# The compression's weight units between those of the queries' projection, and the first chunk's gates handed to the attention's list of side work

## The chip, the cores and the metric

One Trainium2 chip, and one of its cores. The metric is device time in microseconds (us) of one execution of the whole program. The kernel before has a median of 2008.77 us over 3 runs.

## What is computed

One step of a decoder layer with the same weights for two groups: a prompt of 1024 tokens, and 8 sequences of 8 new tokens each over a paged cache of 2048 (the sample). Width is 1024; all is float32. Cut to what the change touches, for the prompt:

```
h   = rmsnorm(x) * (1 + scale) + shift
zq, zk, zv, za, zr, zqn, zkv, zg = split(h @ w_in)     # one input projection
o_g = rmsnorm(gla(zq, zk, zv, za)) * silu(zr)          # gated linear attention, zr are its gates
kc  = silu(windows(zkv[0]) @ w1[0] + b1) @ w2[0] + b2  # compression: 63 blocks of 32 tokens
vc  = silu(windows(zkv[1]) @ w1[1] + b1) @ w2[1] + b2
o_n = g0 * attn(zqn, kc, vc) + g1 * attn(zqn, selected k, v) + g2 * attn(zqn, window k, v)
x   = x + gt * rmsnorm(concat(o_g, o_n) @ w_out)       # then a squared-ReLU MLP
```

## The kernel before

Tokens lie on the free axis, in three chunks: 384, 384 and 256 prompt tokens with the 64 sample tokens (`CHUNKS`). Each float32 operand of a product is split into a high part, rounded by ScalarE (`split`, L248), and the rest, subtracted by VectorE (L249). A product is then three matmuls (`mm3`, L254 to L256).

Weights come in units of 512 KB (`wunit`, L261). SyncE (SP in the profile) loads a unit into one of 3 buffers `wr`; ScalarE makes `wh` and VectorE `wl`, each with 2 buffers. So a `wh` buffer is free again when TensorE has ended the unit before last, and a `wr` buffer when the `wl` of its unit is made. SP works in order: a load that waits for a buffer holds all loads behind it.

The program is written stage by stage, and the compiler's scheduler then fixes one order for each engine. `main_phase` calls in turn:

- `project_kv`: keys and values of the three branches, written to DRAM (`kvd`, `vd`). At its end POOL starts two copies of the sample's window state from DRAM to DRAM (L803, L804).
- `keys_values`: first the compression. For each kind (keys, values) it loads one row of `kvd` (L1024), splits it, and multiplies it with 4 weight units `cw1` of 12 matmuls each into one accumulator in PSUM's `mm` banks. A tanh, two transposes and a small product make `KC` and `VC`. Then it loads the keys and values of the other two branches (`k32`, `v32`, one buffer each, L1081 and L1085) and splits them into `KK` and `VV`.
- `project_q`: 4 units `w_f`, each over the three chunks (72 matmuls), written to `qd`.
- `project_gate`: 4 units over chunks two and three (48 matmuls each), then the same 4 units, loaded again, over chunk one (24 each). Each result passes a tanh (L760) and two VectorE operations (L761, L763) that multiply it into `catg`; POOL writes that to DRAM (`cgd`).
- `attention`: prompt tiles of 128 tokens in 16 passes. For each of the 8 heads TensorE makes scores against `KC`, `KK[1]` and `KK[0]` (L1122, L1123), VectorE adds the mask and takes the maximum (L1125), ScalarE the exponential (L1129), POOL scales (L1135), TensorE transposes (L1145) and multiplies with the values (L1148, L1149).

While the attention runs, a generator (`sample`) gives side work: the sample's own attention, in `SAMPLE_WORK` = 122 steps over the first three of four parts, as many as the done share of the attention's width asks for:

```python
while done < min(1, work / total(i)) * STEPS[i == 3]:
    done += next(between, 1e9)
```

Of the kernel before, what the change touches and what calls it, by code (L numbers as in the profile page):

```python
# [17 lines left out]
NP = 1024  # L18
# [9 lines left out]
SAMPLE_WORK = 10 + 4 * 28  # L28
# [188 lines left out]
class Prog:  # L217
# [320 lines left out]
    def hidden(self, i):  # L538
        c0, npr, n = CHUNKS[i]
        hp = self.pool(self.right, f"hT{c0}", side="right")  # L540
        self.xs.append(tuple(self.t(hp, [128, 8, n], F32R, f"hT{k}") for k in range(2)))
# [74 lines left out]
    def main_phase(self):  # L616
        nc, tc, a = self.nc, self.tc, self.a
        ffn = ExitStack()
        with ExitStack() as top:
            with ExitStack() as left, self.right as right:  # L620
                self.catg = self.t(self.pool(right, "cat", side="right"), [128, 4, NT], F32, "catg")
# [10 lines left out]
                next(project_gla)  # L632
                for i in (1, 2):
                    self.hidden(i)
# [21 lines left out]
            between, work, done = self.sample(), 0, 0  # L656
# [97 lines left out]
    def project_gate(self, pool, xs):  # L754
        nc, a = self.nc, self.a

        for cis, i in product((slice(1, 3), slice(0, 1)), range(4)):
            for ps, (c0, npr, n) in zip(self.feat_linear(a["w_f"][4 + i], 128, xs[cis]), CHUNKS[cis]):
# [3 lines left out]
                cat = self.catg[:, i, c0:c0 + n]  # L762
# [12 lines left out]

# [46 lines left out]
    def gla(self, st):  # L822
# [11 lines left out]
        for i in range(8):  # L834
# [75 lines left out]
            nc.scalar.mul(self.catg[:, :, cols], pt.rearrange("p (h t) -> p h t", h=4), self.small[:, 32:33])  # L910
# [18 lines left out]
    def gla_sample(self, pool):  # L929
# [52 lines left out]
        nc.vector.scalar_tensor_tensor(self.catg[:, :, NP:], v(oT), self.small[:, 32:33], v(r), op0=OP.mult, op1=OP.mult)  # L982
# [27 lines left out]
    def keys_values(self, st):  # L1010
# [6 lines left out]
        with ExitStack() as st2:  # L1017
            pool = self.pool(st2, "cmp")
            t = lambda shape, tag, bufs=1, dt=F32: self.t(pool, shape, dt, tag, bufs)
            nb = 63  # L1020
            M = 2 * nb
            for kind in range(2):
                x32 = t([128, NP], "x32", 2)
                nc.sync.dma_start(x32, self.kvd[kind, :, :NP])  # L1024
                xh, xl = (t([128, 8, 64, 2], x, 1, F32R) for x in ("xh", "xl"))
                for h in range(2):
                    for j2 in range(2):
                        src = x32[64 * h:64 * h + 64].rearrange("p (c j i) -> p i j c", j=8, i=2)[:, j2]
                        self.split(*(y[64 * j2:64 * j2 + 64, :, :, h] for y in (xh, xl)), src)
                ps = self.bank("mm")[:M, :256]  # L1030
                xs = [y.rearrange("p j c h -> p j (c h)") for y in (xh, xl)]
                for u in range(4):
                    h, l = self.wunit(a["cw1"][kind, u], 4, 256)
                    for i in range(4):
                        k = 4 * u + i
                        o = 2 * (k // 8)
                        self.mm3(ps, (xs[0][:, k % 8, o:o + M], xs[1][:, k % 8, o:o + M]), (h[:, i], l[:, i]),
                                 k == 0, False)
                nc.tensor.matmul(ps, self.C("ones")[:3, :M], self.brow[:, kind], start=False, stop=True)
                e = t([128, 256], "ce", 2)[:M]  # L1040
                nc.scalar.activation(e, ps, AF.Tanh, scale=0.5)
                nc.vector.scalar_tensor_tensor(e, e, 1.0, ps, op0=OP.add, op1=OP.mult)
                nc.vector.tensor_scalar(e, e, 0.5, None, op0=OP.mult)
                pt = self.bank("g")[:, :2 * M].rearrange("p (a b) -> p a b", a=2)
                for f in range(2):
                    nc.tensor.transpose(pt[:, f], e[:, f * 128:(f + 1) * 128], self.C("ident")[:M, :M])
                hh, hl = (t([128, 2, M], x, 2, F32R) for x in ("chh", "chl"))
                self.split(hh, hl, pt)
                if kind == 0:
                    pk = self.bank("g")[:, :M]  # L1050
                    for f in range(2):
                        self.mm3(pk, (self.cw2h[:, 0, f], self.cw2l[:, 0, f]), (hh[:, f], hl[:, f]), f == 0, f == 1)
                    b2 = self.small[:, 33:34]
                    for h in range(2):
                        src = pk.rearrange("p (c h) -> p h c", h=2)[:, h]
                        dst = self.KC[:, h, :, :nb]
                        nc.vector.tensor_scalar(dst[:, 0], src, b2, None, op0=OP.add)
# [513 lines left out]
```

## Time and profile before

| | |
|---|---|
| median of 3 runs | 2008.77 us (2002.26 to 2010.27) |
| profiled execution, its own time | 2006.12 us |
| its span, first to last instruction | 2004.5 us |
| mean granted clock of TensorE | 0.952 of full speed |
| TensorE busy | 1864.0 us (93% of the span) |
| VectorE busy | 1111.7 us (55%) |
| ScalarE busy | 799.0 us (40%) |
| POOL busy | 410.8 us (20%) |

How to read it: a busy TensorE is not one at full speed. Its granted clock has two levels, 1.2 and 2.4 GHz, which the views show as 0.50 and 1.00; a value between is a mean over a stretch with both. Idle time of any engine costs something only where TensorE, or the engine that bounds that stretch, waits for it. PE is TensorE's matmul, DVE VectorE, ACT ScalarE, SPq SyncE's issue of transfers.

### The profile page before, as it was taken

The page shows a single profiled execution, that of the slowest core. Times are in us where ns is not written, and L with a number is a line of the kernel's source. Part 1 is how long each engine was busy: PE and PEld are TensorE (multiplying, and loading weights), DVE is VectorE, ACT ScalarE, POOL GpSimd, SP SyncE. Part 2 cuts the span into 40 slices and gives each one's busy share as a digit, 9 for nine tenths or more (in the row PEclk, how much of TensorE's full clock was granted, in tenths as well). Part 3 has the DMA queues.
Part 4 walks back from the last instruction along what each step waited for, and adds up shares of the span by engine and source line. Part 5 has one row for each costly group of instructions (what it writes and reads, how often), then busy time and mean ns, then how long its engine had stood idle before and what let it go on. Part 6 is the DMA issues. An engine that isn't in the chain of part 4 may idle for free.

```text
span 2004.5 us, 33005 instructions
## 1 busy us (share of the span) xinstructions
PE 1864.0 (93%) x12033; PEld 1711.5 (85%) x12033; DVE 1111.7 (55%) x2493; ACT 799.0 (40%) x1646; POOL 410.8 (20%) x660
## 2 busy tenths in 40 slices
PE   4989999999979989999998879999999999999995
PEld 3878889999969866576796878989999999999995
DVE  7757765364533596677768757633333333333347
ACT  4324353253332475566756635432302121212153
POOL 3433202134401344444312013000000000000024
PEclk9999999999969898899999889999999999999998
DMA  7567641013543503333212476551111111111125
GB/s 248 177 223 252 208 129 53 22 38 123 176 166 119 173 6 97 108 108 106 80 53 69 151 226 221 199 172 63 43 42 53 43 43 43 48 48 43 43 76 176
DMA packets 107624, 223.93 MB, mean 112 GB/s; under 512 B 12763, under 2 KB 68477, under 8 KB 106022
## 3 DMA queue, kind: packets, MB, share of 16 engines
q1 hardware_dynamic: 91814, 172.07, 26.9%
q0 software_dynamic: 13920, 47.53, 7.0%
q8 instruction: 94, 1.54, 0.3%
q10 hardware_dynamic: 1728, 2.23, 0.3%
q14 instruction: 68, 0.56, 0.1%
HBM read 190.72 MB, written 35.19 MB: 113 GB/s over the span
## 4 chain that ended last, share of the span: by engine, by line
PE 76%; DVE 10%; DMA 6%; issue 3%; ACT 2%; POOL 1%; SPq 1%; POOLq 0%; ACTq 0%; DVEq 0%
PE mm L255 13%; PE mm L254 13%; PE mm L256 13%; PE dn L254 6%; PE dn L255 6%; PE dn L256 6%; PE g L1145 3%; DMA wr<-w_ada 2%; PE av L1148 2%; PE dn L1122 2%; PE av L1149 2%; PE dn L1123 1%; DVE wl L249 1%; PE g L882 1%; PE mm L1296 1%
## 5 line engine op out<-in xcount | busy, mean ns | idle before, releaser
L248 ACT CAST wh<-wr 128x1024 fp32r<-128x1024 f32 (+1 forms) x152 | 158.2, 1041 | 444.7 <-PE dn L255 273.1
L249 DVE TENSOR_TENSOR wl<-wr,wh 128x1024 fp32r<-128x1024 f32 (+1 forms) x144 | 177.6, 1234 | 205.5 <-ACT wh L248 205.2
L254 PE MATMUL mm<-fh,wh 128*128 128x384 f32 (+1 forms) x768 | 254.1, 331 | 13.0 <-DMA fh<-h2d 13.0
L254 PE MATMUL dn<-fh,wh 128*128 128x384 f32 (+1 forms) x768 | 253.9, 332 | 7.3 <-DVE fo L1513 3.4
L255 PE MATMUL mm<-fl,wh 128*128 128x384 f32 (+1 forms) x768 | 254.5, 331 | 3.3 <-DMA fl<-h2d 3.3
L256 PE MATMUL mm<-fh,wl 128*128 128x384 f32 (+1 forms) x768 | 253.1, 331 | 1.6 <-DVE wl L249 1.1
L255 PE MATMUL dn<-fl,wh 128*128 128x384 f32 (+1 forms) x768 | 253.4, 330 | 0.1
L256 PE MATMUL dn<-fh,wl 128*128 128x384 f32 (+1 forms) x768 | 252.7, 330 | 0.0
L1513 DVE TENSOR_TENSOR fo<-fo,dn 128x384 f32<-128x384 f32 (+1 forms) x168 | 88.9, 530 | 190.7 <-PE dn L256 189.8
L254 PEld LDWEIGHTS mm<-fh,wh 128*128 128x128 f32 x768 | 145.6, 190 | 13.5 <-issue 12.0
L254 PEld LDWEIGHTS dn<-fh,wh 128*128 128x128 f32 x768 | 144.4, 188 | 10.9 <-ACT fh L248 4.6
L551 POOL TENSOR_TENSOR acc<-acc,sq 128x384 f32<-128x384 f32 x14 | 18.7, 1338 | 653.9 <-ACT sq L550 653.6
L255 PEld LDWEIGHTS mm<-fl,wh 128*128 128x128 f32 x768 | 145.5, 189 | 4.1 <-DMA fl<-h2d 4.1
L256 PEld LDWEIGHTS mm<-fh,wl 128*128 128x128 f32 x768 | 145.5, 190 | 2.2 <-DVE wl L249 1.4
L255 PEld LDWEIGHTS dn<-fl,wh 128*128 128x128 f32 x768 | 144.7, 188 | 1.2 <-DVE fl L249 1.2
L256 PEld LDWEIGHTS dn<-fh,wl 128*128 128x128 f32 x768 | 144.6, 188 | 0.0
L254 PE MATMUL mm<-hT,wh 128*128 128x384 f32 (+3 forms) x408 | 138.0, 338 | 1.8 <-ACT st L771 1.8
L255 PE MATMUL mm<-hT,wh 128*128 128x384 f32 (+3 forms) x408 | 136.9, 336 | 0.0
L256 PE MATMUL mm<-hT,wl 128*128 128x384 f32 (+3 forms) x408 | 136.9, 335 | 0.0
L249 DVE TENSOR_TENSOR pl<-g,ph 128x512 fp32r<-128x512 f32 (+3 forms) x148 | 99.9, 684 | 21.3 <-ACT ph L248 13.9
L248 ACT CAST ph<-g 128x512 fp32r<-128x512 f32 (+3 forms) x148 | 83.4, 583 | 62.9 <-PE g L1145 40.6
L1493 DVE TENSOR_TENSOR u<-u 128x384 f32<-128x384 f32 (+1 forms) x96 | 56.6, 590 | 87.5 <-ACT u L1492 87.5
(470 smaller groups left out, 4608.7 us busy)
## 6 DMA issues: line engine op xcount, KB each, us to landing
wr<-w_down SPq DMA_DIRECT2D x52, 512.0 KB, 3.5
wr<-w_ada SPq DMA_DIRECT2D x48, 512.0 KB, 4.8
wr<-w_up SPq DMA_DIRECT2D x44, 512.0 KB, 3.5
wr<-w_f SPq DMA_DIRECT2D x24, 512.0 KB, 3.6
wr<-cw SPq DMA_DIRECT2D x16, 512.0 KB, 4.5
raw<-cc SPq DMA_DIRECT2D x64, 128.0 KB, 4.2
raw<-cc POOLq DMA_DIRECT2D x64, 128.0 KB, 4.6
wr<-w_out SPq DMA_DIRECT2D x16, 512.0 KB, 3.6
```

Source lines behind the costliest of these rows:

```text
L248: return (self.nc.scalar.copy(h, src), (lo or self.nc.vector).tensor_tensor(l, src, h.bitcast(F32), op=OP.subtract))
L249: (lo or self.nc.vector).tensor_tensor(l, src, h.bitcast(F32), op=OP.subtract))
L254: mm(out, ah, bh, start=start, stop=False)
L255: mm(out, ah, bl, start=False, stop=False)
L256: mm(out, al, bh, start=False, stop=stop)
L882: nc.tensor.matmul(pa[:, p, j], KI[:, j].rearrange("p a b -> p (a b)"), QB[:, p, j], start=True, stop=True)
L1122: nc.tensor.matmul(ps, q, K[:, 0, c:c + cw], start=True, stop=False)
L1145: nc.tensor.transpose(pt[:, 128 * g:128 * g + 128], S[g][:, c:c + cw], self.C("ident"))
L1148: nc.tensor.matmul(av, V, ph, start=first and c == 0, stop=False)
L1149: nc.tensor.matmul(av, V, pl, start=False, stop=last and c + 128 >= width)
L1493: nc.vector.tensor_tensor(u, u, u, op=OP.mult)
L1513: nc.vector.tensor_tensor(o, o, ps, op=OP.add)
```

## The change

Three things. The compression becomes a generator (`compressed_keys`) that gives control back after every two weight units, and the queries' projection takes one such piece after each of its own units; its accumulator moves from the `mm` to the `dn` banks. The loads of `KK` and `VV` become a function of their own, called after the queries. The gates of chunk one leave the projection and become the first four steps of the attention's side work (now 126), so their inputs stay allocated until then; for that `catg` becomes two tiles, and the inputs of chunks two and three get a stack of their own.

```diff
-SAMPLE_WORK = 10 + 4 * 28
+SAMPLE_WORK = 4 + 10 + 4 * 28
...
+    def cat(self, c0, n):
+        x, o = (self.catg[0], 0) if c0 < CHUNKS[1][0] else (self.catg[1], CHUNKS[1][0])
+        return x[:, :, c0 - o:c0 - o + n]
...
-            with ExitStack() as left, self.right as right:
-                self.catg = self.t(self.pool(right, "cat", side="right"), [128, 4, NT], F32, "catg")
+            right = top.enter_context(self.right)
+            self.catg = [self.t(self.pool(right, "cat0", side="right"), [128, 4, CHUNKS[0][2]], F32, "catg0")]
+            with ExitStack() as left, ExitStack() as mid:
...
-                self.keys_values(kvs)
-                self.project_q(proj, xs)
-                self.project_gate(proj, xs)
-            self.cmp_stack.close()
+                with ExitStack() as st:
+                    steps = self.compressed_keys(kvs, st)
+                    for _ in self.project_q(proj, xs):
+                        next(steps)
+                self.load_keys(kvs)
+                for _ in self.project_gate(proj, xs, slice(1, 3)):
+                    pass
...
-            between, work, done = self.sample(), 0, 0
+            between, work, done = self.fillers(proj, xs, right), 0, 0
...
-        for cis, i in product((slice(1, 3), slice(0, 1)), range(4)):
+        for i in range(4):
...
+            yield 1
...
-                ps = self.bank("mm")[:M, :256]
+            ps = self.bank("dn")[:M, :256]
...
+                if u == 1:
+                    yield
...
+    def fillers(self, proj, xs, right):
+        yield from self.project_gate(proj, xs, slice(0, 1))
+        right.close()
+        self.cmp_stack.close()
+        yield from self.sample()
```

Since a scheduler sets the order, these are pieces of what it made. SP's loads after those of `project_kv` (`w_f` are units of queries or gates, `cw` of the compression, `k` and `v` the inputs of `KK` and `VV`), before:

```order
L261 DMA wr_7040<-cw 128x1024
L1024 DMA x_912_7009<-kvd_100 128x1024
L261 DMA wr_7058<-cw 128x1024
L1024 DMA x_933_7117<-kvd_100 128x1024
L1081 DMA k_958_7241<-kvd_100 64x1024 x2
L1085 DMA v_960_7251<-vd_102 128x4x128
L261 DMA wr_7076<-cw 128x1024
L261 DMA wr_7130<-cw 128x1024
L261 DMA wr_7148<-cw 128x1024
L261 DMA wr_7166<-cw 128x1024
L261 DMA wr_7184<-cw 128x1024
L261 DMA wr_7286<-w_f 128x1024
```

and now, where the load of the first query unit stands just ahead of this piece:

```order
L261 DMA wr_7117<-cw 128x1024
L1037 DMA x_922_7104<-kvd_100 128x1024
L261 DMA wr_7135<-cw 128x1024
L1037 DMA x_961_7394<-kvd_100 128x1024
L1100 DMA k_995_7609<-kvd_100 64x1024 x2
L1104 DMA v_997_7619<-vd_102 128x4x128
L261 DMA wr_7153<-w_f 128x1024
L261 DMA wr_7244<-cw 128x1024
L261 DMA wr_7262<-cw 128x1024
L261 DMA wr_7303<-w_f 128x1024
L261 DMA wr_7407<-cw 128x1024
L261 DMA wr_7425<-cw 128x1024
```

One unit of the queries now stands before each pair of the compression's. TensorE's order follows: 72 matmuls of a query unit around or before 24 of the compression. Of the second to fourth pair of `k` and `v` loads, which stood among the query units, all now stand behind the four gate units of chunks two and three and two of chunk one.

ScalarE's order at the second pair of compression units, in the changed kernel (`st` is a query result leaving PSUM, `wh_7154` and `wh_7304` are the second and third query units, the other three `wh` compression units):

```order
L783 ACTIVATE st_7062<-mm_7037,cst_66 128x384
L248 CAST wh_7136<-wr_7135 128x1024
L248 CAST wh_7154<-wr_7153 128x1024
L248 CAST wh_7245<-wr_7244 128x1024
L783 ACTIVATE st_7090<-mm_7065,cst_66 128x320
L783 ACTIVATE st_7184<-mm_7159,cst_66 128x384
L248 CAST wh_7263<-wr_7262 128x1024
L783 ACTIVATE st_7212<-mm_7187,cst_66 128x384
L248 CAST wh_7304<-wr_7303 128x1024
```

Before, the casts of the compression's units followed each other, with nothing but its own small steps between them. Now each second one takes the buffer that a query unit leaves.

TensorE at the first scores of the attention (`KC`, `QS`), in the changed kernel; `hT`, `wh`, `wl` are the third unit of chunk one's gates:

```order
L254 MATMUL mm_8157<-hT_458_3824,wh_8152 128x384
L1141 MATMUL dn_7944<-KC_7097,QS_7933 128x24
L1142 MATMUL dn_7944<-KC_7097,QS_7933 128x24
L255 MATMUL mm_8157<-hT_459_3825,wh_8152 128x384
L1141 MATMUL dn_7949<-KC_7097,QS_7933 128x24
L1142 MATMUL dn_7949<-KC_7097,QS_7933 128x24
L256 MATMUL mm_8157<-hT_458_3824,wl_8153 128x384
```

Before, the first such scores stood between the second and the third unit; now they stand inside the third. All 96 gate matmuls of chunk one still come ahead of the first score against `KK`, and the sample's first score has moved from row 3660 of TensorE's order to row 3700, its last from 4728 to 4767.

## Rows read from the trace of the kernel before

**Rows 1.** The page's first part, busy us (share of the span) xinstructions, and of its second the clock granted to TensorE in 40 equal slices, in tenths.

```profile
PE 1864.0 (93%) x12033; PEld 1711.5 (85%) x12033; DVE 1111.7 (55%) x2493; ACT 799.0 (40%) x1646; POOL 410.8 (20%) x660
PEclk9999999999969898899999889999999999999998
```

**Rows 2.** Busy time by stretch. Columns: start:end and length in us, then PE, PEld, DVE, ACT, POOL busy us (xinstructions), granted clock, DMA share, GB/s.

```profile
540.00:580.00 40.00, 24.24 (x108) 20.57 (x108) 17.22 (x22) 14.67 (x17) 4.77 (x8) 0.61 0.64 222
596.00:684.00 88.00, 83.87 (x503) 82.92 (x501) 34.49 (x61) 27.36 (x49) 14.62 (x27) 1.00 0.49 152
684.00:764.00 80.00, 71.67 (x317) 51.11 (x317) 62.88 (x215) 49.25 (x140) 35.57 (x57) 0.77 0.17 55
764.00:1090.00 326.00, 311.56 (x2056) 234.74 (x2055) 237.84 (x805) 210.75 (x533) 118.88 (x189) 0.96 0.28 88
```

**Rows 3.** What TensorE waited for between 539.7 and 685 us: us in total, times, longest.

```profile
PE mm L254 <- ACT wh L248: 7.2, 3, 3.7
PE mm L255 <- DVE wl L249: 4.8, 6, 2.0
PE mm L254 <- ACT xh L248: 3.7, 1, 3.7
PE dn L1122 <- DVE mx L1125: 2.4, 1, 2.4
PE mm L254 <- ACT st L771: 1.8, 2, 1.6
```

**Rows 4.** Busy time by stretches of 5 us, columns as in rows 2.

```profile
540.00:545.00 5.00, 3.48 (x17) 3.29 (x18) 2.64 (x4) 2.44 (x4) 4.66 (x8) 0.73 0.55 161
545.00:550.00 5.00, 4.41 (x32) 4.00 (x32) 3.01 (x3) 2.50 (x3) 0.11 (x1) 0.93 1.00 381
555.00:560.00 5.00, 2.99 (x12) 2.40 (x11) 0.71 (x1) 0.21 (x1) 0.00 (x0) 0.50 0.69 293
575.00:580.00 5.00, 3.57 (x13) 2.91 (x13) 2.51 (x3) 0.82 (x1) 0.00 (x0) 0.50 0.49 138
580.00:585.00 5.00, 5.00 (x20) 4.78 (x20) 1.85 (x3) 0.61 (x2) 0.00 (x0) 0.68 0.51 179
615.00:620.00 5.00, 3.40 (x23) 3.09 (x22) 1.90 (x3) 2.61 (x5) 1.07 (x2) 1.00 0.56 200
```

**Rows 5.** The same columns for four stretches of unbroken matmuls: the last tiles of `project_kv` (256 columns each), one query unit, the four gate units over chunks two and three, two gate units over chunk one.

```profile
528.86:539.78 10.92, 10.92 (x93) 10.66 (x91) 0.84 (x2) 1.26 (x4) 5.80 (x10) 1.00 0.72 242
621.00:633.00 12.00, 12.00 (x74) 12.00 (x73) 1.33 (x2) 2.63 (x4) 1.62 (x3) 1.00 0.26 89
633.00:664.04 31.04, 31.04 (x194) 31.04 (x193) 12.12 (x19) 7.59 (x12) 4.32 (x8) 1.00 0.39 131
664.04:672.60 8.56, 8.56 (x52) 8.56 (x50) 6.56 (x10) 5.24 (x9) 0.54 (x1) 1.00 0.63 182
```

**Rows 6.** TensorE in order of time: start us, us, engine line op out<-in xcount, and in brackets its idle time before and what ended it. The last matmul of `project_kv`, the first two waits of the compression, a wait in the queries' projection, the first score against `KC` after the gates and the first against `KK`.

```profile
539.50 0.28 PE L256 MATMUL mm<-wh,hT 128*64 128x256 f32 x1
...
540.64 0.38 PE L254 MATMUL mm<-wh,xh 128*126 128x256 f32 x1 [0.86 <-ACT wh L248]
541.90 0.38 PE L255 MATMUL mm<-wl,xh 128*126 128x256 f32 x1 [0.88 <-DVE wl L249]
...
617.38 0.42 PE L254 MATMUL mm<-hT,wh 128*128 128x320 f32 x1 [1.60 <-ACT st L771]
...
683.96 0.28 PE L1122 MATMUL dn<-KC,QS 128*128 128x24 f32 x1 [2.36 <-DVE mx L1125]
...
684.64 0.44 PE L1122 MATMUL dn<-KK,QS 128*128 128x384 f32 x1
```

**Rows 7.** The weight buffers `wr` between 540 and 570 us: the cast and the subtraction of a unit (ns min/median/max), and the time from a load's issue to its landing.

```profile
L248 ACT CAST wh<-wr x8: 1044/1046/1049, 539.5 to 569.1; 128x1024 fp32r<-128x1024 f32 x8
L249 DVE TENSOR_TENSOR wl<-wr,wh x7: 1218/1225/1226, 540.6 to 568.9; 128x1024 fp32r<-128x1024 f32 x7
DMA to landing us min/median/max: 3.7/10.6/18.3
```

**Rows 8.** Transfers issued between 540 and 570 us (line engine op xcount, KB each, median us to landing), and POOL's issue of the two copies (start us, us).

```profile
wr<-cw SPq DMA_DIRECT2D x5, 512.0 KB, 13.0
wsk<-swk POOLq DMA_DIRECT2D x1, 2016.0 KB, 13.3
wsv<-swv POOLq DMA_DIRECT2D x1, 2016.0 KB, 22.5
...
543.76 0.78 POOL L803 DMA_DIRECT2D wsk<-swk  x1
544.53 0.57 POOL L804 DMA_DIRECT2D wsv<-swv  x1
```

**Rows 9.** ScalarE's casts of the second to fourth key halves, in order of time, with the idle time before each.

```profile
599.93 1.05 ACT L248 CAST KK<-k 128x1024 fp32r<-128x1024 f32 x1 [3.69 <-DMA k<-kvd]
608.19 1.05 ACT L248 CAST KK<-k 128x1024 fp32r<-128x1024 f32 x1 [4.22 <-DMA k<-kvd]
615.18 1.05 ACT L248 CAST KK<-k 128x1024 fp32r<-128x1024 f32 x1 [3.96 <-DMA k<-kvd]
```

**Rows 10.** Three stretches of the attention, columns as in rows 2.

```profile
684.64:704.00 19.36, 18.63 (x63) 13.79 (x64) 11.84 (x56) 9.89 (x34) 8.45 (x17) 0.53 0.37 126
724.00:764.00 40.00, 33.09 (x148) 22.13 (x146) 34.19 (x91) 23.23 (x58) 20.48 (x28) 0.83 0.13 39
844.00:884.00 40.00, 38.19 (x279) 27.46 (x277) 28.36 (x106) 27.16 (x66) 21.13 (x32) 1.00 0.45 136
```

More of the change, by code (lines that the diff above doesn't have):

```diff
@@ L632, in main_phase @@
                 next(project_gla)
+                cat = self.pool(mid, "cat", side="right")
+                self.catg.append(self.t(cat, [128, 4, NT - CHUNKS[1][0]], F32, "catg"))
                 for i in (1, 2):
-                    self.hidden(i)
+                    self.hidden(i, mid)
                 with ExitStack() as st:
@@ new lines, in compressed_keys @@
+        pool = self.pool(st2, "cmp")
+        t = lambda shape, tag, bufs=1, dt=F32: self.t(pool, shape, dt, tag, bufs)
+        nb = 63
+        M = 2 * nb
+        for kind in range(2):
+            x32 = t([128, NP], "x32", 2)
+            nc.sync.dma_start(x32, self.kvd[kind, :, :NP])
+            xh, xl = (t([128, 8, 64, 2], x, 1, F32R) for x in ("xh", "xl"))
+            for h in range(2):
+                for j2 in range(2):
+                    src = x32[64 * h:64 * h + 64].rearrange("p (c j i) -> p i j c", j=8, i=2)[:, j2]
+                    self.split(*(y[64 * j2:64 * j2 + 64, :, :, h] for y in (xh, xl)), src)
+            ps = self.bank("dn")[:M, :256]
+            xs = [y.rearrange("p j c h -> p j (c h)") for y in (xh, xl)]
+            for u in range(4):
+                h, l = self.wunit(a["cw1"][kind, u], 4, 256)
+                for i in range(4):
+                    k = 4 * u + i
+                    o = 2 * (k // 8)
+                    self.mm3(ps, (xs[0][:, k % 8, o:o + M], xs[1][:, k % 8, o:o + M]), (h[:, i], l[:, i]),
+                             k == 0, False)
+                if u == 1:
+                    yield
+            nc.tensor.matmul(ps, self.C("ones")[:3, :M], self.brow[:, kind], start=False, stop=True)
+            e = t([128, 256], "ce", 2)[:M]
+            nc.scalar.activation(e, ps, AF.Tanh, scale=0.5)
+            nc.vector.scalar_tensor_tensor(e, e, 1.0, ps, op0=OP.add, op1=OP.mult)
+            nc.vector.tensor_scalar(e, e, 0.5, None, op0=OP.mult)
+            pt = self.bank("g")[:, :2 * M].rearrange("p (a b) -> p a b", a=2)
+            for f in range(2):
+                nc.tensor.transpose(pt[:, f], e[:, f * 128:(f + 1) * 128], self.C("ident")[:M, :M])
+            hh, hl = (t([128, 2, M], x, 2, F32R) for x in ("chh", "chl"))
+            self.split(hh, hl, pt)
+            if kind == 0:
+                pk = self.bank("g")[:, :M]
+                for f in range(2):
+                    self.mm3(pk, (self.cw2h[:, 0, f], self.cw2l[:, 0, f]), (hh[:, f], hl[:, f]), f == 0, f == 1)
+                b2 = self.small[:, 33:34]
+                for h in range(2):
+                    src = pk.rearrange("p (c h) -> p h c", h=2)[:, h]
+                    dst = self.KC[:, h, :, :nb]
+                    nc.vector.tensor_scalar(dst[:, 0], src, b2, None, op0=OP.add)
+                    nc.vector.scalar_tensor_tensor(dst[:, 1], src, b2, dst[:, 0].bitcast(F32),
+                                                   op0=OP.add, op1=OP.subtract)
+            else:
+                pv = self.bank("g")[:nb, :128]
+                for h in range(2):
+                    for f in range(2):
+                        x = [y[:, f].rearrange("p (c h) -> p h c", h=2)[:, h] for y in (hh, hl)]
+                        self.mm3(pv[:, 64 * h:64 * h + 64], x, (self.cw2h[:, 1, f, :64], self.cw2l[:, 1, f, :64]),
+                                 f == 0, f == 1)
+                v32 = t([64, 128], "cv32")[:nb]
+                nc.vector.tensor_tensor(v32, pv, self.small[:nb, 34:162], op=OP.add)
+                d = self.VC[:nb].rearrange("p h (i d) -> p i h d", i=2)
+                self.split(d[:, 0], d[:, 1], v32.rearrange("p (h d) -> p h d", h=2))
+            yield
```

67 lines of the change are left out of this document (9 added, 58 removed).

## The prediction, before the changed kernel was run

> **What bounds the kernel now.** I began with the page's first part: TensorE is busy 93% of the span, no other engine over 55% [rows 1]. So time is to be had only where TensorE stands still or runs below full speed, and the 40 slices show where to look: in nearly all of them the granted clock reads 9; it dips in two places, near 40% and near 60% of the span [rows 1]. The busy time by stretch says what these are. Between 540 and 580 us, the compression, TensorE is busy 24.24 of 40 us at a clock of 0.61, and no other engine is busier; between 684 and 764, the attention's start, the clock is 0.77 with VectorE at 62.88 of 80 us; between 596 and 684, mostly queries and gates, it is 83.87 of 88 at 1.00 [rows 2]. Next the waits of TensorE from 539.7 to 685: 20.2 us in all, the largest on `wh` (7.2) and `wl` (4.8) of the weight units and on the compression's input `xh` (3.7) [rows 3]. And the clock in steps of 5 us: 0.93 at 545, 0.50 at 555 and still 0.50 at 575, 0.68 at 580 [rows 4]. The compression has 12 matmuls for a weight unit that costs a cast of 1.05 and a subtraction of 1.22 us [rows 7], so it waits at each unit, and its low clock lasts into the next stage.
>
> **What the change is worth, by the stage it rewrites.** The stage reaches from 539.7 (last matmul of the keys and values) to the first score against `KK` at 684.64 [rows 6]: 144.9 us. I take its TensorE work at full clock from stretches without a gap [rows 5]:
>
> - four query units of 12.00: 48.0
> - the gates of chunks two and three: 31.0
> - four chunk-one gate units at half of 8.56: 17.1
> - 96 compression matmuls at 10.92/93, a stretch of the same 256 columns: 11.3
> - transposes, bias and small products of the compression: 3.5 (an estimate: some 30 matmuls, at a price near 10.92/93 each)
>
> That makes 110.9. Of the other 34.0, 20.2 are the waits; the last 13.8 is the half clock, which fits some 28 us (from 555 to 583) at 0.50 [rows 4].
>
> None of this work is removed: the change has the same units, loads and splits. It moves 12 us query units between pairs of compression units. The wait for `xh` goes (it is loaded while a query unit runs), and so do nearly all those for `wh`. **What remains**, followed along the new order:
>
> - The first `wh` and `wl` at the stage's head: 0.86 and 0.88, as now [rows 6].
> - Each second compression unit's cast waits until TensorE has left the query unit ahead (its buffer of `wh`), so `wl` is there 1.05 + 1.22 = 2.27 us later [rows 7], while the partner unit offers cover of at most 11 matmuls (1.3 us). That gives about 0.95, 2.15 (one matmul of cover), 0.3 and 0.95: 4.4.
> - One wait for a result to leave PSUM, since ScalarE's casts of `KK` now stand among the gates: 1.45, by the 1.60 at 617.38 now [rows 6].
>
> Sum 7.5. All could be covered (0) or stay as large as they are now (20.2); I take 7.5 because each is built from a measured cast. For the clock after such waits there is no row at exactly this mix. Between 540 and 545, after gaps of 0.86 and 0.88, it was 0.73; between 615 and 620, with a gap of 1.60, it stayed 1.00 [rows 4]. So a wait costs between 0 and about 1.4 us (0.27 of 5) of low clock; I take two such dips, 2.8. The first `KC` scores between the gates: 1.3. So the stage takes 110.9 + 7.5 + 2.8 + 1.3 = 122.5 us: **22.4 less**.
>
> **The chunk-one gates as side work** bring TensorE little by themselves: all 96 matmuls still stand ahead of the first `KK` score, and only the first `KC` scores now stand among the last of them. The 2.36 us wait for `mx` there [rows 6] gets cover (counted above). The tanh, the products and the write to `cgd` stay ahead of the sample's work as before. The sample's first matmul moves 40 rows of TensorE's order later, its last 39; at 406 us for 2373 matmuls in the attention [rows 2] that is some 7 us at either end: the same work, shifted within a stage that goes on to 1090. Cost 0; if the work behind it had no cover, up to 7.
>
> **The attention's start.** Its first 19.36 us run at 0.53 [rows 10], after 3 us in which TensorE stood still or did little [rows 6]. Now the scores follow full-width gate matmuls without that pause. At clock 1.00 the 18.63 busy us would take 9.9: a gain between 0 and 8.7. A loss is not excluded, since 724 to 764 also reads only 0.83 [rows 10], but nothing in the change lowers it further. I take 3, nearer to nothing, since VectorE's share is high in this stage [rows 2] and would partly hold the time. The Trainium skill ("TensorE: Matmul & The Clock Gate", Part 4: PE-mode transpose) says that transposes do not count as busy for raising the clock; the attention is full of them, and by that this term would be 0 and the time 3 us longer. The trace does not settle it: 844 to 884, with the attention's transposes in the mix, runs at 1.00 [rows 10].
>
> **Loads.** A unit lands in 3.7 us at best, but 10.6 in the median and 18.3 at worst between 540 and 570 [rows 7], when POOL's two copies of 2016 KB, issued at 543.76 and 544.53, take 13.3 and 22.5 us [rows 8]. The copies stay where they are. Now the loads have 12 us of query matmuls to land in: the third compression unit, issued near 543, is needed near 560; the fourth, issued near 556, near 571. At 18.3 us these would be some 2 and 3.7 late, at the median of 10.6 neither is. I cost it at 0. The loads of `KK` and `VV` now start near 618, behind six weight units; at 7 to 8 us per half (599.93, 608.19, 615.18 [rows 9]) three of them end near 642, and the first `KK` score comes near 662: 0, with some 16 us to spare.
>
> **Sum.** −22.4 − 3 = −25.4. The profiled execution has 2006.12 us, so 1980.7 of its own time. The median is 2.65 above it, which would give 1983.4; I say **1982**.
>
> **Rivals.**
>
> - *Weights late beside the copies.* The loads issued near 543 and 556 share the DMA with the copies, and the worst landing of now repeats: some 6 us of waits and about 5 us of half clock behind them (as the stretch after 555 now has, though shorter [rows 4]). Gain 14: 1994. For it: 18.3 and 22.5 us landings [rows 7, 8]. Against: these loads now queue fewer at a time. The Trainium skill ("DMA: Bandwidth & Descriptors", Queues, rings and completion order) says each DMA engine takes turns between the queues it has work for, packet by packet, which would make a lone load suffer less than a share of the copies' size suggests. Chance 0.14.
> - *The attention starts at full clock.* The term of 3 becomes 8.7, and the dips stay away (2.8): gain 34, 1974, or 1970 if the small waits go too. For: 596 to 684 at 1.00 just ahead [rows 2]. Against: VectorE, 62.88 of 80 [rows 2]. Chance 0.08.
> - *Given back in the attention.* The sample's work is later by some 7 us and ends over work that VectorE bounds; the casts of `KK`, `VV` and chunk one's products meet there too. Gain 22.4 less 7 at each end: about 2001. For: VectorE at the attention's start [rows 2]. Against: 764 to 1090 has TensorE busy 311.56 of 326 [rows 2], so the order of equal work matters little. Chance 0.08.
> - *Slower: the half clock spreads over the mix.* The mechanism is the one of 555 to 583, where gaps of about 2 to 4 us [rows 3] keep the clock at 0.50. If the four gaps of 1 to 2 us keep it low through the 59 us of queries and compression, their work takes up to 59 more; half of them at 0.50 cost 30. It decides from 25 us on, when the gain is gone; at 30 the time is 2013. For: 0.73 after gaps of 0.86 and 0.88. Against: 0.93 between 545 and 550 and 1.00 after a gap of 1.60 [rows 4]; the query units are unbroken 12 us stretches. Chance 0.04.
>
> That the change doesn't do what it says is out: the new order shows the interleaving on SP, ScalarE and TensorE.
>
> **How the numbers follow.** The forecast's own case, 0.66, reaches from 1971 to 1989 (waits between nearly none and 13, attention start between 0 and 8). With most of the first two rivals the range is 1968 to 1996; it leaves out the last two and the tails. A measurement of this kernel tells about 0.5%, 10 us, from no change. The forecast and the first two rivals are all faster by more, 0.88, less 0.02 for their slow tail: faster 0.86, same 0.08 + 0.02 = 0.10, slower 0.04.
>
> **What would show it.** Right: between 540 and 660 no wait of TensorE over 2.5 us, a clock of 1.00 but for short dips, the first `KK` score near 662 instead of 684.64, and an attention from there on as long as now or up to 9 us shorter. Wrong, by step: casts of `wh` that wait for a load `wr` (the first rival); stretches of 0.50 among the query units (the last); the first score early, but more waits on VectorE or ScalarE in the 400 us behind it (the third); waits for `KK` or `VV` from their loads (the slack of 16 us).

## The result and the profile after

The changed kernel has a median of 1987.35 us over 7 runs (1981.11 to 1993.26), the kernel before, run beside it, 2007.16 (1995.82 to 2012.63): a ratio of 0.9908, 95% interval 0.9879 to 0.9938, some 19 us. A second series of the same kernel gave 1986.45 and 0.9930 (0.9896 to 0.9963). The forecast of 1982 was 5 us too low, inside its range. The profiled execution took 1989.29 us, its span 1987.6.

The page's first part and the clock over 40 slices, to be read beside [rows 1]:

```profile
PE 1860.6 (94%) x12033; PEld 1712.3 (86%) x12033; DVE 1109.1 (56%) x2493; ACT 800.7 (40%) x1646; POOL 411.3 (21%) x660
PEclk9999999989999888999998989999999999999998
```

The same work is done. Busy time by stretch (columns as in [rows 2]): the stage from the last key and value matmul to the first score against `KK`, from there to the last matmul of the first output projections (called the attention below), the rest from the first MLP matmul on (between the last two lie some 14 us of norms, 9 with the gates alone); then two pieces of the stage and the attention's first 19.36 us.

```profile
540.35:664.10 123.75, 115.55 (x709) 112.45 (x708) 55.24 (x91) 47.94 (x78) 19.14 (x35) 0.99 0.58 183
664.10:1150.20 486.10, 453.48 (x2839) 352.29 (x2839) 357.93 (x1153) 307.11 (x776) 166.88 (x260) 0.92 0.30 93
1164.80:1987.60 822.80, 790.90 (x4676) 782.85 (x4676) 365.60 (x630) 233.54 (x397) 58.08 (x45) 0.98 0.27 88
...
565.00:570.00 5.00, 3.53 (x13) 3.53 (x14) 1.42 (x2) 2.04 (x3) 1.08 (x2) 0.72 0.44 173
570.00:575.00 5.00, 5.00 (x32) 5.00 (x31) 0.00 (x0) 0.58 (x1) 0.54 (x1) 0.94 0.42 142
...
664.10:683.46 19.36, 17.25 (x72) 12.93 (x72) 12.81 (x53) 13.97 (x43) 10.55 (x20) 0.74 0.51 177
```

The stage took 145.1 us before (539.50 to 684.64, [rows 6]) and takes 123.8. The clock is 0.99; its one dip is at 565, where before the clock stood at 0.50 from 555 to some 583 [rows 4]. The attention and the MLP did not gain: 484.6 and 821.0 us before, 486.0 and 822.8 now. What TensorE waits for in the stage, beside [rows 3]:

```profile
PE mm L254 <- DVE st L772: 2.5, 2, 1.3
PE mm L254 <- ACT st L783: 2.3, 1, 2.3
PE dn L255 <- DVE wl L249: 2.0, 3, 0.8
PE mm L254 <- ACT wh L248: 0.8, 1, 0.8
PE mm L256 <- DVE wl L249: 0.6, 1, 0.6
```

8.2 us instead of 20.2. (L772 is VectorE's first product of a gate, L783 ScalarE's copy of a query result out of PSUM into a buffer `st`, from where it goes to `qd`.) The largest single wait, 2.31, is new, and its chain shows in the order of time (columns as in [rows 6]):

```profile
544.51 0.78 POOL L816 DMA_DIRECT2D wsk<-swk  x1
545.28 0.57 POOL L817 DMA_DIRECT2D wsv<-swv  x1
547.71 0.59 POOL L784 DMA_DIRECT2D qd<-st  x1 [1.85 <-ACT st L783]
...
565.89 0.53 ACT L783 ACTIVATE st<-mm,cst 128x320 f32<-128x320 f32 x1 [6.30 <-DMA qd<-st]
...
566.47 0.44 PE L254 MATMUL mm<-hT,wh 128*128 128x384 f32 x1 [2.31 <-ACT st L783]
```

The views of the tiles `qd` (the writes of the queries) and `wr` (the weight loads) between 540 and 570 us, each with its time from issue to landing:

```profile
DMA to landing us min/median/max: 2.2/8.8/18.2
```

```profile
DMA to landing us min/median/max: 3.4/6.0/9.7
```

And the two copies in the list of transfers (KB, us to landing):

```profile
wsk<-swk POOLq DMA_DIRECT2D x1, 2016.0 KB, 10.8
wsv<-swv POOLq DMA_DIRECT2D x1, 2016.0 KB, 19.5
```

A write of 192 KB that elsewhere lands in 2.2 us took 18.2: POOL issued it at 547.71, behind the two copies, so that it landed at 565.9. ScalarE stood 6.3 us for its buffer, TensorE 2.31 us for ScalarE, and the dip at 565 follows. The weight loads, slow before (18.3 at worst, [rows 7]), now land in 9.7 at worst, and no cast, subtraction or matmul waits for them.

### The profile page after: what moved, and what is told of

Read it like the earlier page. It is cut to its first block, busy times and chain, and to the rows that moved or that the text cites. A ratio compares the mean times of both kernels' runs of the same rounds, so it can differ in the third digit from the quotient of the medians.

```text
span 1987.6 us, 33002 instructions
## 1 busy us (share of the span) xinstructions
PE 1860.6 (94%) x12033; PEld 1712.3 (86%) x12033; DVE 1109.1 (56%) x2493; ACT 800.7 (40%) x1646; POOL 411.3 (21%) x660
## 4 chain that ended last, share of the span: by engine, by line
PE 74%; DVE 9%; issue 8%; DMA 5%; POOL 2%; ACT 1%; SPq 1%; POOLq 0%; DVEq 0%; ACTq 0%
PE mm L255 12%; PE mm L254 12%; PE mm L256 12%; PE dn L254 6%; PE dn L255 6%; PE dn L256 6%; PE g L1164 3%; PE dn L1141 2%; PE av L1167 2%; PE dn L1142 2%; PE av L1168 2%; DMA wr<-w_ada 1%; DMA xt<-xT 1%; PE g L895 1%; PE mm L1315 1%
## 5 line engine op out<-in xcount | busy, mean ns | idle before, releaser
L254 PE MATMUL mm<-hT,wh 128*128 128x384 f32 (+3 forms) x408 | 140.3, 344 | 5.6 <-DVE st L772 2.5
L255 PE MATMUL mm<-hT,wh 128*128 128x384 f32 (+3 forms) x408 | 138.8, 340 | 0.0
```

Of the source, the lines that this page charges most:

```text
L254: mm(out, ah, bh, start=start, stop=False)
L255: mm(out, ah, bl, start=False, stop=False)
```

## The experiments

All of them in one table: medians and ratios to the kernel before on the same chips, and from one profile each the lengths of the stage, the attention and the MLP as bounded above (starts of the instructions named there; in us).

| kernel | median us | ratio (95%) | stage | attention | MLP |
|---|---|---|---|---|---|
| before | 2007.16 | 1 | 145.1 | 484.6 | 821.0 |
| changed | 1987.35 | 0.9908 (0.9879 to 0.9938) | 123.8 | 486.0 | 822.8 |
| changed, again | 1986.45 | 0.9930 (0.9896 to 0.9963) | 125.7 | 484.1 | 822.9 |
| interleave only | 1992.66 | 0.9942 (0.9916 to 0.9969) | 121.9 | 490.8 | 821.6 |
| gates only | 1999.78 | 0.9973 (0.9947 to 0.9999) | 138.8 | 495.5 | 813.9 |
| before, copies in the attention | 2025.12 | 1.0084 (1.0054 to 1.0114) | 127.8 | 505.3 | 820.8 |
| changed, copies in the attention | 2009.80 | 1.0009 (0.9985 to 1.0033) | 120.7 | 509.4 | 821.0 |
| before, copies in the MLP | 1984.64 | 0.9880 (0.9852 to 0.9909) | 128.3 | 487.8 | 811.5 |
| changed, copies in the MLP | 2003.68 | 0.9977 (0.9962 to 0.9993) | 121.2 | 498.4 | 820.9 |
| changed, copies on ScalarE's queue | 2003.30 | 0.9979 (0.9955 to 1.0002) | 121.1 | 501.8 | 822.4 |
| changed, query writes by ScalarE | 1995.48 | 0.9959 (0.9933 to 0.9985) | 121.6 | 493.6 | 820.8 |
| changed, copies behind the query writes | 1987.99 | 0.9918 (0.9886 to 0.9949) | 123.9 | 483.0 | 823.0 |
| interleave only, copies in the MLP | 1979.15 | 0.9862 (0.9837 to 0.9886) | 124.6 | 485.4 | 820.0 |
| the same, norms first | 1973.74 | 0.9832 (0.9798 to 0.9866) | 121.0 | 485.1 | 811.3 |

The start of the last key and value matmul, ahead of all this, lies between 531.7 and 544.8 us in these profiles, though TensorE's order up to there is the same in all (it was 539.5 before; 540.4 and 531.7 in two executions of the changed kernel). So a single execution tells about 6 us either way of the whole; the lengths of the parts tell more, though the stage of one and the same order, too, was 123.8 and 125.7 us (the changed kernel) and 124.6 and 121.0 (the last two) in two executions. One row needs care: of the twelve runs of the kernel before with its copies in the attention, three took 2004 to 2006 us and nine 2023 to 2032. Its profile and lengths are of one of the three; where the other nine lose 20 us more no trace shows, only that their mean clock is 0.942 to 0.947, not 0.956 or 0.957.

**One half at a time.** Interleave only:

```diff
...
-                for _ in self.project_gate(proj, xs, slice(1, 3)):
-                    pass
+                for cis in (slice(1, 3), slice(0, 1)):
+                    for _ in self.project_gate(proj, xs, cis):
+                        pass
...
-            between, work, done = self.fillers(proj, xs, right), 0, 0
+            between, work, done = self.sample(), 0, 0
```

> The change without its second half: chunk one's gates stay in the projection, the compression still lies between the query units. Theory 'interleave' (the gain comes from TensorE having query matmuls to run while the compression's units are loaded and split: waits 20.2 -> 9.9 us and half clock 13.8 -> 1.7 us in the stage that ends at the first KK score): about 19 us below the kernel before, within 4 us of the whole change; stage near 124 us instead of 144.9. Rival 'gates' (the handing over of the gates starts the attention better): at most 12 us below.

Gates only:

```diff
-                    steps = self.compressed_keys(kvs, st)
-                    for _ in self.project_q(proj, xs):
-                        next(steps)
+                    for _ in self.compressed_keys(kvs, st):
+                        pass
                 self.load_keys(kvs)
+                for _ in self.project_q(proj, xs):
+                    pass
...
-            ps = self.bank("dn")[:M, :256]
+            ps = self.bank("mm")[:M, :256]
```

> The change without its first half: the compression runs as one block again, ahead of the queries; chunk one's gates are side work of the attention. Theory 'interleave': within 4 us of the kernel before (at best the 2.36 us wait at the first scores goes); stage 142 to 146 us. Rival 'gates': 8 us or more below the kernel before.

The stage's gain is the interleave's: 121.9 us with it alone. (The 9.9 us of waits in the expectation count 1.7 at the attention's start; up to the first `KK` score they are 8.2.) The whole fell by 14 us where 19 was expected, and the attention took 490.8. The gates alone took 6 us off the stage, to 138.8 where 142 to 146 was expected, 2.4 of them the wait for `mx` [rows 3], and lost 11 in the attention; the median fell by 6.5 where 4 at most was expected, in part for a reason that comes below (the MLP took 813.9).

**Is it the cover, or the copies?** The copies moved out of the compression, in both kernels, to the end of the attention's first part (issued by POOL behind its scaling, L1154 of the changed kernel):

```diff
-        with self.tc.issue_after(last.ins):
-            nc.gpsimd.dma_start(a["wsk"][:, :, :504], a["swk"][:, :, 8:])
-            nc.gpsimd.dma_start(a["wsv"][:, :504], a["swv"][:, 8:])
...
+                if i == 1:
+                    with tc.issue_after(self.scale.ins):
+                        nc.gpsimd.dma_start(a["wsk"][:, :, :504], a["swk"][:, :, 8:])
...
```

> The kernel before with the two DRAM copies of 2016 KB moved from the compression's start into the attention, nothing else. Theory 'interleave' in its narrow form (the compression waits because 12 matmuls do not cover a cast of 1.05 and a subtraction of 1.22 us): only the wait for the second input (3.7 us) and some of the waits behind slow loads go; up to 6 us below before, clock still 0.50 around 555 to 580. Rival 'copies' (the compression waits for loads that land late beside the copies, 10.6 us in the median; where loads are there in time the waits are only 0.19 and 0.40 us, as at 546 to 549): loads land in some 4 us, most of the waits and of the half clock go, 12 to 20 us below before.

> The whole change with the same move of the two copies. Theory 'POOL queue': in the changed kernel the copies stand ahead of the first writes of query results on POOL's queue; one such write landed after 18.2 us (median 2.2), ScalarE waited 6.3 us for its buffer, TensorE 2.31 us and then 1.7 us of low clock. Without them: about 4 us below the change, stage 119 to 120 us instead of 123.5, no result that waits for a write. Rival (the wait is ScalarE's order, not the write): no difference over 1.5 us.

Both forecasts of the whole were missed, by over 20 us: 12 to 20 below the kernel before was expected of the one, and it came out 19 above; 4 below the change of the other, and it came out 22 above. The lengths show two things. The kernel before has a stage of 127.8 instead of 145.1, so the rival was right there, and in the changed kernel the wait for the query result is gone, with a stage of 120.7 at a clock of 1.00. And the attention pays. In the kernel before, POOL's issues of the sample's page loads waited behind the copies, and the work behind these issues with them; a small load on SP's queue (`vc`, issued at 735.67) landed after 19.0 us where the median is 2.4. TensorE's two longest waits there follow (start us, us, and idle time):

```profile
732.83 0.83 POOL L669 DMA_DIRECT2D wsk<-swk  x1
...
744.34 0.55 POOL L240 DMA_DIRECT2D wr<-ckv  x1 [4.28 <-DMA wsk<-swk]
753.94 0.55 POOL L240 DMA_DIRECT2D wr<-ckv  x1 [9.05 <-DMA wsv<-swv]
...
754.78 0.70 PE L1340 MATMUL mm<-vc,PT 128*64 128x128 f32 x4 [7.58 <-DMA vc<-vcs]
...
761.70 0.71 PE L1146 MATMUL g<-cst,Sc 128*8 128x128 f32 x2 [5.17 <-POOL Sc L1136]
```

The share of the DMA engines in use had been low there, 0.13 between 724 and 764 [rows 10]; what the copies met was work that waits for its loads. So they went into the middle of the MLP, where the share is 0.14 as well but TensorE has no gap (496 of 496 us busy from 1408 to 1904 in the kernel before), and onto ScalarE's queue, since POOL has no instruction there to stand behind:

```diff
...
             hids = up(ch, range(3))
+            if ch == 3:
+                with self.tc.issue_after(self.relu.ins):
+                    nc.scalar.dma_start(a["wsk"][:, :, :504], a["swk"][:, :, 8:])
+                    nc.scalar.dma_start(a["wsv"][:, :504], a["swv"][:, 8:])
```

> The kernel before with the two copies issued by ScalarE in the middle of the MLP, where TensorE has no gap and the DMA share is 0.15; nothing else. With the copies in the attention the stage had shrunk from 145 to 128 us, but the attention grew by 20, since the sample's page loads on POOL's queue waited 4.3 and 9.1 us for the copies. Theory 'copies' (most of the compression's loss came from loads beside the copies): stage 126 to 130 us, attention as before, about 16 us below before. Rival (the copies cost as much wherever they lie, or the stage's gain was chance): within 6 us of before.

> The whole change with the copies in the MLP as well. Theory 'copies': stage 120 to 121 us as with the copies in the attention, attention as in the change: 3 to 4 us below the change, some 1983 us; what the interleaving still gives over the kernel before with the same move is then only 7 to 9 us instead of 19. Rival (the interleaving is worth the same 19 us with or without the copies): 16 us or more below the kernel before with the same move, some 1970 us.

With that move alone, and none of the change, the kernel before falls to 1984.64, as low as the changed kernel. Its order of TensorE in the stage is that of before but for 45 of 708 matmuls, and between 1500 and 1550 us, with the copies under way (the DMA share is 0.36 there, 0.16 in the 50 us before), TensorE is busy 50.00 of 50 us. The waits of TensorE in its stage:

```profile
PE mm L254 <- ACT xh L248: 3.7, 1, 3.7
PE dn L1119 <- DVE mx L1122: 2.4, 1, 2.4
PE mm L255 <- DVE wl L249: 1.5, 3, 0.9
PE mm L254 <- ACT st L771: 1.0, 1, 1.0
PE mm L254 <- ACT wh L248: 1.0, 1, 1.0
PE mm L256 <- DVE xl L249: 0.3, 1, 0.3
```

The view of its weight buffers `wr` from 535 to 565 us, and the whole stage by stretch (columns as in [rows 2]):

```profile
DMA to landing us min/median/max: 3.4/3.7/4.6
```

```profile
534.70:662.80 128.10, 117.91 (x707) 114.47 (x706) 56.41 (x93) 48.34 (x79) 19.21 (x35) 0.96 0.48 153
```

The waits for `wh` and `wl` fall from 12.0 [rows 3] to 2.5 with the same casts and subtractions: most of them had been waits for loads. The trace of before says so itself: two of ScalarE's casts, at 559.78 and 567.86, stood idle for the load of their unit. The 3.7 for `xh` stays, since it is no load but four casts in a row on ScalarE. ScalarE in the kernel before, in order of time:

```profile
550.30 4.34 ACT L248 CAST xh<-x 64x512 fp32r<-64x512 f32 x4 [0.89 <-PE mm L255]
559.78 1.04 ACT L248 CAST wh<-wr 128x1024 fp32r<-128x1024 f32 x1 [5.14 <-DMA wr<-cw]
...
567.86 1.04 ACT L248 CAST wh<-wr 128x1024 fp32r<-128x1024 f32 x1 [6.75 <-DMA wr<-cw]
```

With the copies out of the way the interleave still shortens the stage, 128.3 to 121.2, as expected, by 7 and not by 21. But the whole, 2003.68 against the forecast of 1983, missed by 20 us, 12 of them in the attention.

**The queue.** The copies where they were, but on ScalarE's queue; and, the other way round, the query writes on ScalarE's queue and the copies on POOL's:

```diff
-        with self.tc.issue_after(last.ins):
-            nc.gpsimd.dma_start(a["wsk"][:, :, :504], a["swk"][:, :, 8:])
+        with self.tc.issue_after(copied.ins):
+            nc.scalar.dma_start(a["wsk"][:, :, :504], a["swk"][:, :, 8:])
...
-                nc.gpsimd.dma_start(self.qd[:, i, c0:c0 + npr], s[:, :npr])
+                nc.scalar.dma_start(self.qd[:, i, c0:c0 + npr], s[:, :npr])
```

(the first two pairs of lines in the one kernel, the last pair in the other)

> The whole change with the copies where they were, but issued by ScalarE on its own queue instead of POOL's. It tells what held the write of the second query unit's result (18.2 us to landing). Theory 'POOL queue' (the write stands behind the copies in the same queue): it lands in 2 to 5 us, TensorE's wait of 2.31 us for it goes, and the weight loads land as in the change (median 3.8, worst about 10 us); 2 to 4 us below the change. Rival 'bandwidth' (the copies fill the DMA engines, whatever the queue): the write still takes over 10 us and the wait stays.

> The whole change with the writes of the query results issued by ScalarE, so that they no longer stand behind the copies on POOL's queue; the copies stay. Theory 'POOL queue': as with the copies on ScalarE's queue, the write of 18.2 us lands in 2 to 5 us, the 2.31 us wait goes, stage 120.5 to 122 us. What becomes of the whole depends on the attention's new order: 1980 to 1985 if it stays at 486, up to 2000 if it goes to 500 as in the two with moved copies.

TensorE's wait for a query result is gone in both, and the stages are 121.1 and 121.6. But the writes (538 to 575 us) landed after 12.7 and 10.3 us at worst, not 2 to 5:

```profile
DMA to landing us min/median/max: 2.1/5.1/12.7
```

```profile
DMA to landing us min/median/max: 1.7/6.0/10.3
```

So each theory was half right: in a queue other than that of the copies a write comes sooner than 18.2, and the wait goes, but it still lands late beside them. With the copies in the MLP the writes between 540 and 570 us have

```profile
DMA to landing us min/median/max: 2.1/2.2/2.2
```

The whole missed the 2 to 4 us below the change that the first of the two was to bring, by some 19: its attention took 501.8. The second, 1995.48, lies within what its expectation allows.

**The order.** Behind the stage the changed kernel and the two just told have the same work, in other orders, and the attention took 486.0, 501.8 and 493.6 us. The changed kernel once more:

> The changed kernel once more, unaltered, for a second profile of the same order of instructions. From the first KK score to the last matmul of the first output projections the profiles so far read 484.6 us before, 486.0 changed, 490.8 interleave only, 495.5 gates only, and 498.4 and 501.8 for the two with the copies moved, which have one and the same order there. Theory 'order' (each of these edits makes the scheduler reorder some 1000 of TensorE's rows in the attention, and that costs or gives up to 15 us): 484 to 490 again, median near 1987. Rival 'chance' (one execution differs from the next by so much there): anywhere between 484 and 502.

484.1 against 486.0. The changed kernels with the copies in the MLP and on ScalarE's queue, which have one and the same order of TensorE there, took 498.4 and 501.8. So, as far as two profiles of each tell, the length follows the order, not chance. The changed kernel with its copies in the attention has that order too, but for 4 of 2838 matmuls, and took 509.4: of the 23 us that it lost there 8 to 11 are the copies, the rest the order. In two stretches of 150 us from the first `KK` score on (columns as in [rows 2]), the changed kernel, then those two:

```profile
664.12:814.12 150.00, 136.73 (x751) 95.93 (x752) 112.70 (x437) 97.96 (x299) 69.36 (x130) 0.86 0.30 93
814.12:964.12 150.00, 143.81 (x933) 100.96 (x930) 112.04 (x382) 99.19 (x234) 61.11 (x92) 0.95 0.29 88
```

```profile
664.94:814.94 150.00, 135.75 (x727) 94.58 (x726) 107.62 (x419) 94.57 (x290) 69.90 (x130) 0.83 0.30 93
814.94:964.94 150.00, 139.87 (x889) 97.21 (x888) 107.30 (x360) 94.06 (x215) 55.93 (x85) 0.95 0.25 77
```

```profile
665.88:815.88 150.00, 136.86 (x717) 94.90 (x717) 106.31 (x413) 94.97 (x290) 69.08 (x127) 0.80 0.29 91
815.88:965.88 150.00, 140.76 (x887) 96.21 (x888) 107.96 (x364) 92.87 (x210) 56.39 (x88) 0.95 0.25 77
```

Both fall behind in the first stretch by the clock (0.83 and 0.80 against 0.86) and in the second by gaps; but the kernel before, at 0.81 and 1.00 in the same two, lost nothing on the whole. Which step of the order costs the time is open: set side by side in order, 601 of the attention's 2838 matmuls stand elsewhere. Nor does every other order cost: between before and the changed kernel 800 do, and the lengths agree within 1.4 us.

The copies behind the last query write, which gives an attention in an order nearer to that of before (242 of 2838 matmuls stand elsewhere):

```diff
+        with self.tc.issue_after(last.ins):   # last: the last write of project_q
+            nc.gpsimd.dma_start(a["wsk"][:, :, :504], a["swk"][:, :, 8:])
+            nc.gpsimd.dma_start(a["wsv"][:, :504], a["swv"][:, 8:])
```

> The whole change with the copies issued by POOL behind the last write of query results, beside the gates (31 us of unbroken matmuls, units of 7.8 us). POOL's order in the attention is then nearly that of the kernel before (19 rows of difference). Theory 'copies': the queries' and the compression's part of the stage is as with the copies moved away; two buffers of gate units cover loads of 10 us, not of 18, so 0 to 5 us of new waits for weights: stage 120 to 126. Theory 'order': the attention near 485 as before. Together 1978 to 1987. Rival 'copies cost wherever DMA is wanted': the loads of KK and VV, which now run beside them, come too late and the stage is over 128.

As expected, 483.0 and 123.9; the median, 1987.99, is a little over the 1978 to 1987 given.

**Towards a better kernel.** Interleave only with the copies in the MLP. In the attention 11 of its 2838 matmuls stand elsewhere than in the kernel just told, against 806 for the order that took 498.4 and 501.8 us (this is what the expectation's second sentence is about):

> The first half of the change alone (the compression between the query units, chunk one's gates in the projection) with the copies in the MLP. TensorE's order in the attention then differs by 24 rows from that of the change with the copies behind the query writes, where it took 483.0 us, and by 1051 or more from none of the slow ones is it closer. Theory 'order': attention 482 to 487, stage 119 to 122 (as interleave only, without its 1.3 us wait for a result's write): 23 to 27 us below before, about 1980 us, the fastest so far. Rival (moving the copies away costs the attention some 12 us by itself, as it did in the two before): attention 495 to 502, about 1995 us.

1979.15, attention 485.4. The rival, that moving the copies costs the attention by itself, is out. The stage, 124.6, missed the 119 to 122 given: its clock was 0.97, where the same order in the next kernel ran at 1.00 and took 121.0. The MLP had shown two lengths, too: 811.5 and 813.9 in the two kernels named below, 820 to 823 in the others. Last, therefore:

```diff
             for k in (2, 3):
-                self.wout_norms(wps[k], "g", x2[k - 2], *PARTS[k])
+                with tc.high_priority(offset=2000):
+                    self.wout_norms(wps[k], "g", x2[k - 2], *PARTS[k])
```

> The interleave with the copies in the MLP, and the scheduler told to place the norms behind the last output projection (tiles of 256 prompt and 64 sample tokens) ahead of other work. In the kernel with only the copies moved to the MLP, and in the one with the gates alone, the stretch from the first MLP matmul to the end took 811.5 and 813.9 us, in all others 820 to 823; in the orders the two differ from the others in that the small products of these norms stand ahead of the first down-projection matmuls, not among them. Here the order in the MLP's start becomes the same, and the attention's stays as it was. Theory 'order': 811 to 814 us from the first MLP matmul on, attention 483 to 487, in all 7 to 10 us below the same kernel without this edit (1979.15): 1969 to 1972. Rival 'chance': 820 to 823, no difference in the whole.

1973.74 us, the lowest median of all, 2 over the 1969 to 1972 given; stage 121.0, MLP 811.3, and the attention, in the same order as without the edit, 485.1. What TensorE waits for in the MLP's first 200 us or so, without that edit and with it:

```profile
PE mm L254 <- DMA fh<-h2d: 13.1, 2, 12.2
PE mm L255 <- DMA fl<-h2d: 3.3, 2, 2.6
PE dn L254 <- ACT fh L248: 3.0, 3, 1.7
```

```profile
PE mm L254 <- DMA fh<-h2d: 11.7, 1, 11.7
PE mm L255 <- DMA fl<-h2d: 1.6, 1, 1.6
PE dn L254 <- ACT fh L248: 1.3, 3, 0.5
```

The 12.2 and the 11.7 lie ahead of the first MLP matmul, outside the length; the rest of these lines is 7.2 us without the edit and 2.9 with it, and the clock of the first 150 us rises from 0.95 to 0.98. The norms make the last MLP inputs; with the last of their small products 64 us into the MLP, not 80, these inputs are there earlier. Such an order, not the copies' place, gave 9.5 of the 22 us of the kernel before with its copies in the MLP, and 7 us of the kernel with the gates alone: both have these products ahead, and the changed kernel with its copies in the MLP, which has not, took 820.9.

## Why the prediction was right, and where it was not

- **The stage: right in size.** 122.5 forecast, 123.8 and 125.7 measured. In the first of these, waits 8.2 against 7.5, low clock 1.7 (0.28 and 0.06 of 5 us each) against 2.8; the rest is work, 113.8 against 112.2.
- **The waits: right in sum, not in kind.** Those for `wl` behind a query unit came to 2.0, not 4.4. 2.5 us for VectorE's products of the gates (`st`, L772) were not foreseen. The result that leaves PSUM late was, but at another place: the step "one wait for a result, since ScalarE's casts of `KK` stand among the gates" failed. It was the query unit's write behind the copies on POOL's queue. The prediction walked SP's queue past the copies for the weights and left out that the moved query units issue writes on POOL's.
- **What bounds the compression: wrong.** "12 matmuls for a cast of 1.05 and a subtraction of 1.22, so it waits at each unit." The kernel before with its copies elsewhere has the same 12 matmuls, casts and subtractions, and waits 2.5 us for `wh` and `wl` in place of 12.0. 17 of the 21 us that the stage could win were loads beside the copies. The row for it was there: landings of 10.6 in the median and 18.3 at worst [rows 7], and 0.93 of the clock between 545 and 550, where the loads had come in time [rows 4]. Nearest of all was ScalarE's idle time before its casts: 11.9 us until a load `wr` had landed, beside the 12.0 that TensorE waited for `wh` and `wl`. The size came out all the same because 12 us of query matmuls cover a load of up to 9.7 us as well as a cast; the prediction had counted on that cover for the loads, but not seen that it was most of the gain. So far the right size is luck.
- **The gates: nearly right.** Stages of 123.8 and 125.7 with them as side work and 121.9 without: they bring the stage nothing that shows. The wait for `mx` ahead of the first `KK` score is gone without them too.
- **The attention's start: wrong.** 3 forecast, nothing measured: 486.0 and 484.1 against 484.6. The clock of the first 19.36 us did rise, from 0.53 [rows 10] to 0.74, with 72 matmuls instead of 63 in them, and the lead was lost again in the attention. The rule of the Trainium skill ("TensorE: Matmul & The Clock Gate", Part 4: PE-mode transpose) would have put this term at 0, which it was; but the clock did rise there, and that transposes took the gain away no run here shows.
- **The loads of `KK`: right.** The last cast of `KK` began at 644.27 and its subtraction ended at 646.6, 17 us ahead of the first score; some 16 were forecast.
- **The rivals.** Weights late beside the copies: they were not, 9.7 us at worst under a cover of 12. The attention starts at full clock: it did not, 0.74. Given back in the attention: not in this kernel, but in others with the same edit and another order (12 to 16 us). Against this rival stood that "the order of equal work matters little", since TensorE is busy 311.56 of 326 us [rows 2]; that was wrong. Half clock through the mix: the clock fell once, to 0.72 and 0.94 in two stretches of 5 us.

The 5 us between forecast and result are the attention's start (3), 1 of the stage, and 1 that lies within the spread of the runs.

## What to carry to other kernels

When small weight units wait, look first at how long their loads take to land and what else the DMA carries there; moving a bulk copy can give most of what reordering the work gives (17 of 21 us here). A low share of busy DMA is not enough for its new place: it was 0.13 in the attention and 0.14 in the MLP, and the copies cost 8 to 11 us in the one, where loads on their own and on other queues are waited for, and nothing that shows in the other. When work is moved, follow its writes too, on the queue of the engine that issues them. And under a scheduler, compare the lengths of the parts that an edit should not touch: here their order changed with nearly every edit and was worth up to 16 us in the attention (486.0 against 501.8) and 9 in the MLP, nearly as much as the edit itself.

## What was not expected of the chip

A write of 192 KB took 18.2 us behind two copies of 2016 KB in the same queue, still 10.3 and 12.7 at worst in another queue beside them, and 2.2 at most between 540 and 570 us without them. A load that usually lands in 2.4 us took 19.0 on SP's queue beside the same copies in the attention. And one execution differs from the next by some 13 us before the stage begins (531.7 to 544.8), in the same order of TensorE's instructions: in the stretch from 393 to 531 us, with TensorE busy over 137 of 138 us each time, the granted clock was 0.96 before, 0.91 in the first profile of the changed kernel and 0.98 in the second.
